# Down projection of a gated MLP with tokens on the partitions, and the residual turned for it

## The chip, the cores and the metric

One core of a Trainium2 chip runs the kernel. Its engines work side by side: PE (matmul; PEld are its weight loads), DVE (VectorE), ACT (ScalarE), POOL (GpSimd) and SP (which issues transfers). The metric is device time in microseconds, the median of three runs.

## The reference, cut to what matters

One encoder layer on 512 tokens of 2048 features, all in float32. The part that the change touches is the end:

```python
x = x + einsum("bsc,cd->bsd", mixed, w_out)          # residual after the mixers
up = einsum("bsd,df->bsf", rms_norm(x, ffn_norm_g), w_up)   # 2048 -> 2 * 5632
gate, val = split(depthwise_conv(up, ffn_dw_w, ffn_dw_b), 2)
x = x + einsum("bsf,fd->bsd", silu(gate) * val, w_down)     # 5632 -> 2048
return rms_norm(x, final_norm_g)      # x * rsqrt(mean(x*x over the 2048) + eps) * g
```

## The kernel before, in words

Everything is kept turned: features on the 128 partitions, the 512 tokens (`S`) along the free axis. `KD` = 16 blocks of 128 features make up a token's 2048. Float32 products are made of three matmuls in a reduced format, with each operand split in a high and a low part (`whi`, `wlo` for weights, `hh`, `hl` for activations): high by high, high by low, low by high. Splitting a 128 x 1024 piece of weights (a *unit*) is one copy on ACT and one subtraction on DVE. Units are loaded by SP into seven buffers (`raw`, `NR` = 7), split into four (`NW` = 4), and asked for three units ahead of their use (`AHEAD` = 3, function `weights`).

The MLP loop runs over `NCH` = 11 groups of `CH` = 4 hidden blocks. Each hidden block `f` is made by seven products (`up`; `pu`), each 8 matmuls of 512 columns and 8 low ones of 256 in one PSUM bank, and by a depthwise convolution and the gate (`hidden`). Between the products stand units of the down projection of the group before (`down`, called after products 3 and 6 through `between`). A unit there is two of the 16 output feature blocks: weights stationary, `hh` and `hl` of 512 tokens moving, four hidden blocks summed in a PSUM bank (`pd`). ACT copies the bank to `pdc`, and POOL adds it to the residual in DRAM by an accumulating transfer (`xd`, shown as `x2d`), 16 feature blocks in all, each [128 features, 512 tokens].

`tick` runs one step of a side job (a Python generator) behind each product; a scheduler then orders each engine's instructions by priority. The order within an engine is fixed when the program is built.

At the end the tenth group's last eight blocks are projected after the last product (`wide`), while the last group's hidden blocks are finished. SP reloads the residual (`reload`, `x2`, lines 830 to 832) and the last weights are split in pieces of 512 columns (`last_weights`, `dh`, `dl`). The eleventh group's projection is done in two halves of 256 tokens (`half`): each adds `pd` to `x2` (L871), squares on ACT (L170), sums the squares over the blocks on DVE (L171). A token's sum of squares then lies across partitions, so `rsqrt_steps` turns it by matmuls with ones (L183), takes the root, and spreads the result over the partitions again with a diagonal and a matmul (L197, L200, `st`). The first half's products with the gain (`finish`, L861) run beside the second half; those of the second half, twelve on DVE and four on POOL, come after it, and eight stores of 256 KB end the program (L862).

Of the kernel before, what the change touches and what calls it, by code (L numbers as in the profile page):

```python
# [16 lines left out]
P = 128  # L17
# [23 lines left out]
H = S // 2  # L41
CH = 4
# [17 lines left out]
         ("nag", NC_), ("g2", KD), ("fww", 2 * NF * 3), ("fwb", 2 * NF), ("g3", KD)]  # L60
# [9 lines left out]
def layer(ctx: ExitStack, tc: tile.TileContext, xT, w_in, w_v, w_out, w_up, w_down, par, tab, out):  # L70
# [94 lines left out]
    def sum_sq(acc, src, first, to=slice(0, S)):  # L165
        if first:
            nc.scalar.activation(acc, src, AF.Square)
        else:
            q = t2("sq")[:, to]
            nc.scalar.activation(q, src, AF.Square)  # L170
            nc.vector.tensor_add(acc, acc, q)  # L171

    def rsqrt_steps(accs, n, name, to=slice(0, S), keep=True, col=None):

        if not isinstance(accs, tuple):
            accs = accs,
        m = (to.stop - to.start) // P
        bank = lambda: (psa.tile([P, 2, S], F32, tag="sc", name="st")[:, 0] if col is None else
                        psa.tile([P, S], F32, tag="po", name="st"))
        ps = bank()  # L180
        for i in range(m):
            for acc in accs:
                nc.tensor.matmul(ps[:, i:i + 1], acc[:, to.start + i * P:to.start + (i + 1) * P], ones[:, 0:1],  # L183
                                 start=acc is accs[0], stop=acc is accs[-1])
        v, r, y = (sm.tile([P, S // P], F32, tag="rs" + c, name="rs" + c)[:, :m] for c in "vry")
        nc.vector.tensor_scalar(v, ps[:, :m], 1.0 / n, EPS, op0=ALU.mult, op1=ALU.add)
# [4 lines left out]
        nc.vector.scalar_tensor_tensor(y, y, 1.5, r, op0=ALU.add, op1=ALU.mult)  # L191
        if col is not None:
            nc.vector.tensor_copy(col, y)
# [6 lines left out]
        nc.tensor.matmul(ps[:, :m * P], ones, dg[:, :m * P], start=True, stop=True)  # L200
        if not keep:
            return ps[:, :m * P]
        res = t2(name)
        nc.scalar.activation(res[:, to], ps[:, :m * P], AF.Copy)
        return res

    def rsqrt_value(g):
        while True:
            try:
                next(g)  # L210
            except StopIteration as e:
                return e.value
# [447 lines left out]
    def down_units(c, i, at):  # L660

        n = U // CH
        if not c:
            return ()
        if c < NCH - 1:
            return {3: (4 * i,), 6: (4 * i + n,)}.get(at, ())
        return {(1, 3): (0,), (1, 6): (2,), (2, 3): (4,), (2, 6): (6,), (3, 6): range(8, KD, n)}.get((i, at), ())

    def down_weights(f0, d0):
        return w_down[:, (f0 * KD + d0 * CH) * P:(f0 * KD + d0 * CH + U) * P]  # L670

    for c in range(NCH):
        for i in range(CH):
            for at, make in enumerate(factors(c * CH + i)):
                plan.append(make)
                for d0 in down_units(c, i, at):
                    plan.append(lambda c=c, d0=d0: unit(down_weights((c - 1) * CH, d0), U * P))

# [122 lines left out]
    def down(hs, ds, wide=False):  # L801

        for d0 in ds:
            w = weights()
            for d in range(d0, d0 + U // CH):

                ps = (psm.tile([P, S], F32, tag="mm", name="pd") if wide and d % 5 > 1 else
                      psa.tile([P, S], F32, tag="tr", name="pd", bufs=2))
                for k in range(CH):
                    mm3(ps, w, (d - d0) * CH + k, *hs[k], k == 0, k == CH - 1)  # L810
                t = t2("pdc")
                nc.scalar.activation(t, ps, AF.Copy)  # L812
                nc.gpsimd.dma_start(xd[d], t, accum_op=ALU.add)  # L813

    pend = None
    for c in range(NCH):
        hs = []
        for i in range(CH):

            last = c == NCH - 1 and i == CH - 1  # L820
            hs.append(hidden(c * CH + i, lambda at: None if last else down(pend, down_units(c, i, at))))
        hs = [in_two(h) for h in hs]
        if not last:
            pend = hs


    n = CH
    x2, ws = [], []

    def reload(d):  # L830
        x2.append(t2("x2"))
        nc.sync.dma_start(x2[d], xd[d])

    def last_weights(d0):
        raw, _ = raw_unit(down_weights(NF - CH, d0), U * P)
        for i in range(2):
            h, l = t2("dh", F32R), t2("dl", F32R)
            o = slice(i * n * P, (i + 1) * n * P)
# [4 lines left out]
    for d in range(KD // 2):  # L843
        reload(d)
    for d in down_units(NCH - 1, CH - 1, 6):
        down(pend, (d,), wide=True)
        last_weights(len(ws))
        last_weights(len(ws))
    for d in range(KD // 2, KD):
        reload(d)  # L850

    def finish(d, r, to, apart=False):

        o = t2("fin").rearrange("p (i t) -> p i t", i=2)
        for i in range(2):
            x, g = x2[d + i][:, to], pc("g3", d + i)
            if apart:
                nc.scalar.activation(x, x, AF.Copy, scale=g)
                nc.gpsimd.tensor_mul(o[:, i], x, r)
# [109 lines left out]
```

## Time and profile before

| | |
|---|---|
| time, median of three runs | 2067.25 us (2064.53, 2067.25, 2067.41) |
| the profiled execution's own time | 2063.7 us |
| its span | 2061.9 us |
| PE busy | 2040.6 us, 99% |
| PEld, DVE, ACT, POOL busy | 1726.8, 1652.3, 1057.5, 156.6 us |
| transfers of `x2d` by POOL | 160 of 256 KB, 4.5 us to landing |
| loads of weights for the MLP | 176 + 88 of 512 KB, 3.6 us to landing |

The span is the profile's; the execution's own time lies 1.8 us above it. Busy time of PE is counted with the overlap of matmuls taken out, so it says that PE was occupied, not that it ran at its peak. The last product of the loop ends at about 1977 us, the last matmul of the projection at 2046.5 us, and what follows is normalisation and stores.

### The profile page before, as it was taken

What the parts mean: (1) busy time and instruction counts of PE and PEld (TensorE: products, weight loads), DVE (VectorE), ACT (ScalarE), POOL (GpSimd) and SP (SyncE); (2) the same over time, 40 slices, a digit from 0 to 9 for tenths busy, and PEclk for the clock granted to TensorE, in tenths of its full rate; (3) what the DMA queues carried; (4) which work ended last, traced back from release to release, by engine and by line L of the source; (5) the groups of instructions that cost most, each with busy time, mean ns of one, the idle gap of its engine ahead of it and who ended that gap; (6) DMA issues with size and microseconds to landing.
All of it is one profiled execution on the core that took longest, in us unless ns stands there. A gap on an engine that the chain in (4) does not pass through costs nothing.

```text
span 2061.9 us, 28498 instructions
## 1 busy us (share of the span) xinstructions
PE 2040.6 (99%) x10746; PEld 1726.8 (84%) x10746; DVE 1652.3 (80%) x2285; ACT 1057.5 (51%) x1714; POOL 156.6 (8%) x186
## 2 busy tenths in 40 slices
PE   9999999999999999999999999999999999999997
PEld 7888888777888998888888888888888888888887
DVE  7798893975577898888888888788788887889876
ACT  7223423466536555555555555555554554555562
POOL 0000000000001001111111111111111111110110
PEclk9999999999999999999999999999999999999998
DMA  6532234325447435555465555555555565554572
GB/s 242 163 103 92 93 115 151 103 72 184 136 144 187 117 123 141 126 143 144 117 150 143 131 135 143 135 131 143 136 134 143 129 144 142 131 137 123 148 210 82
DMA packets 103338, 281.68 MB, mean 137 GB/s; under 512 B 12064, under 2 KB 16672, under 8 KB 103200
## 3 DMA queue, kind: packets, MB, share of 16 engines
q1 hardware_dynamic: 77840, 233.70, 35.7%
q0 software_dynamic: 25216, 46.15, 14.9%
q8 instruction: 85, 1.39, 0.3%
q14 instruction: 53, 0.43, 0.1%
q10 hardware_dynamic: 144, 0.01, 0.0%
HBM read 223.18 MB, written 56.62 MB: 136 GB/s over the span
## 4 chain that ended last, share of the span: by engine, by line
PE 89%; DVE 4%; DMA 3%; issue 2%; ACT 1%; POOL 0%; SPq 0%; DVEq 0%; POOLq 0%; ACTq 0%
PE pu L692 23%; PE pu L693 12%; PE pd L130 8%; PE pd L128 8%; PE pd L129 8%; PE pj L128 5%; PE pj L129 5%; PE pj L130 5%; PE po L128 2%; PE po L129 2%; PE po L130 2%; PE pv L315 1%; PE pv L314 1%; PE pv L316 1%; DMA sq<-sq 1%
## 5 line engine op out<-in xcount | busy, mean ns | idle before, releaser
L692 PE MATMUL pu<-xc,whi 128*128 128x512 f32 x2240 | 782.6, 397 | 0.2 <-ACT pl L706 0.2
L118 DVE TENSOR_TENSOR wlo<-raw,whi 128x1024 fp32r<-128x1024 f32 x364 | 444.7, 1222 | 247.6 <-ACT whi L117 232.1
L117 ACT ACTIVATE whi<-raw 128x1024 fp32r<-128x1024 f32 x364 | 385.1, 1059 | 470.5 <-PE pj L129 130.3
L693 PE MATMUL pu<-xc,wlo 128*128 128x256 f32 x2240 | 583.0, 281 | 0.0
L692 PEld LDWEIGHTS pu<-xc,whi 128*128 128x128 f32 x2240 | 407.8, 188 | 80.3 <-ACT pl L706 0.5
L693 PEld LDWEIGHTS pu<-xc,wlo 128*128 128x128 f32 x2240 | 422.8, 189 | 25.5
L130 PE MATMUL pd<-hh,wlo 128*128 128x512 f32 x640 | 248.9, 391 | 1.4 <-DVE wlo L118 1.4
L128 PE MATMUL pd<-hh,whi 128*128 128x512 f32 x640 | 249.8, 390 | 0.0
L129 PE MATMUL pd<-hl,whi 128*128 128x512 f32 x640 | 249.1, 389 | 0.0
L813 POOL DMA_DIRECT2D x2d<-pdc x160 | 139.6, 874 | 1174.0 <-ACT pdc L812 1072.1
L128 PE MATMUL pj<-xh,whi 128*128 128x512 f32 x512 | 200.5, 396 | 0.2 <-ACT xh L244 0.2
L129 PE MATMUL pj<-xl,whi 128*128 128x512 f32 x512 | 200.4, 391 | 0.1
L130 PE MATMUL pj<-xh,wlo 128*128 128x512 f32 x512 | 200.4, 391 | 0.0
L706 ACT ACTIVATE pl<-pu 128x256 f32<-128x256 f32 x280 | 105.1, 380 | 176.1 <-PE pu L692 176.1
L117 ACT ACTIVATE whi<-ws 128x1024 fp32r<-128x1024 f32 x132 | 139.8, 1059 | 68.5 <-PE pu L692 44.3
L372 DVE SCALAR_TENSOR_TENSOR y<-ch,prm,y 128x510 f32<-128x510 f32 (+14 forms) x240 | 172.0, 743 | 3.5
L118 DVE TENSOR_TENSOR wlo<-ws,whi 128x1024 fp32r<-128x1024 f32 x132 | 161.1, 1220 | 1.4 <-ACT whi L117 1.3
L130 PEld LDWEIGHTS pd<-hh,wlo 128*128 128x128 f32 x640 | 120.1, 188 | 30.0 <-DVE wlo L118 4.9
L812 ACT ACTIVATE pdc<-pd 128x512 f32<-128x512 f32 x160 | 93.9, 588 | 95.4 <-PE pd L130 95.4
L129 PEld LDWEIGHTS pd<-hl,whi 128*128 128x128 f32 x640 | 120.2, 188 | 25.7
L128 PEld LDWEIGHTS pd<-hh,whi 128*128 128x128 f32 x640 | 120.4, 188 | 21.8
L128 PEld LDWEIGHTS pj<-xh,whi 128*128 128x128 f32 x512 | 96.3, 188 | 25.0 <-issue 3.8
(176 smaller groups left out, 2913.7 us busy)
## 6 DMA issues: line engine op xcount, KB each, us to landing
raw<-in_w_up SPq DMA_DIRECT2D x176, 512.0 KB, 3.6
raw<-in_w_down SPq DMA_DIRECT2D x88, 512.0 KB, 3.6
x2d<-pdc POOLq DMA_DIRECT2D x160, 256.0 KB, 4.5
raw<-in_w_in SPq DMA_DIRECT2D x60, 512.0 KB, 3.7
raw<-in_w_out SPq DMA_DIRECT2D x32, 512.0 KB, 3.7
x<-in_xT SPq DMA_DIRECT2D x32, 256.0 KB, 4.3
raw<-in_w_v SPq DMA_DIRECT2D x16, 512.0 KB, 4.8
tab<-in_tab SPq DMA_DIRECT2D x32, 256.0 KB, 4.0
```

The source lines that it names most:

```text
L117: i = nc.scalar.activation(hi[:, :n], raw[:, :n], AF.Copy)
L118: j = nc.vector.tensor_sub(lo[:, :n], raw[:, :n], hi[:, :n].bitcast(F32))
L128: nc.tensor.matmul(ps, hi[:, a], mh, start=start, stop=False)
L129: nc.tensor.matmul(ps, hi[:, a], ml, start=False, stop=False)
L130: return nc.tensor.matmul(ps, lo[:, a], mh, start=False, stop=stop)
L314: nc.tensor.matmul(ps[i], xh, w[0][:, a], start=kk == 0, stop=False)
L372: nc.vector.scalar_tensor_tensor(y[:, a:b], h[:, a + j - PAD:b + j - PAD], prm[:, o + j:o + j + 1], y[:, a:b], op0=ALU.mult, op1=ALU.add)
L692: wide = lambda: nc.tensor.matmul(ps, hi, m, start=k == 0, stop=k == U - 1)
L693: low = lambda: nc.tensor.matmul(ps[:, H:], lo, m[:, :H], start=False, stop=False)
L706: nc.scalar.activation(to, ps, AF.Copy)
L812: nc.scalar.activation(t, ps, AF.Copy)
L813: nc.gpsimd.dma_start(xd[d], t, accum_op=ALU.add)
```

## The change: what it does

The down projection is turned. Hidden activations become the stationary operand, 128 tokens at a time, and 512 columns of weights move; a PSUM bank then holds [128 tokens, 512 features]. The 2048 features are handled in four quarters (`NQ`), four token tiles (`NTT`) each. A quarter takes two units; its four banks are accumulated over both units and copied at the end of the second, and POOL accumulates them into a new DRAM residual `xq[quarter][tile]`. The first group writes `xq` without accumulating.

The residual itself is still made with features on the partitions, so it is turned in a side job, `turn_residual`: per pair of feature blocks SP reloads both, DVE transposes them in blocks of 32 x 32 into one `raw` buffer (`xt`), and SP stores the four bands of 32 partitions to DRAM in runs of 64 elements. The columns of each quarter are chosen (`_quarters`, on the host) so that this regrouping is all that is needed. Then 16 tiles are loaded and accumulated into `xq` by POOL. The job advances with the products of groups 2 to 9.

At the end the tenth group's quarters 2 and 3 are added by DVE straight from PSUM into the reloaded residual, with no copy and no accumulating transfer. The eleventh group goes by token tiles, not by halves: for each quarter DVE adds, ACT squares and accumulates the row's sum in the same instruction, DVE multiplies by the gain (loaded as rows, `g3`). A token's sum is then one number on its partition, so no matmul is needed for the statistics; the root takes the same small steps (`inv_sqrt`), and one scaling per quarter (one on ACT, three on DVE) and one store per quarter finish the tile. The output leaves as [tokens, features] in the quarters' order.

The core of the diff:

```diff
-    def down(hs, ds, wide=False):
-        for d0 in ds:
-            w = weights()
-            for d in range(d0, d0 + U // CH):
-                ps = (psm.tile([P, S], F32, tag="mm", name="pd") if wide and d % 5 > 1 else
-                      psa.tile([P, S], F32, tag="tr", name="pd", bufs=2))
-                for k in range(CH):
-                    mm3(ps, w, (d - d0) * CH + k, *hs[k], k == 0, k == CH - 1)
-                t = t2("pdc")
-                nc.scalar.activation(t, ps, AF.Copy)
-                nc.gpsimd.dma_start(xd[d], t, accum_op=ALU.add)
+    def down3(ps, w, k, hs, kk, i, start, stop):
+        t = slice(i * P, (i + 1) * P)
+        (hi, lo), (h, l) = (x[:, k * S:(k + 1) * S] for x in w[:2]), (x[:, t] for x in hs[kk])
+        nc.tensor.matmul(ps, h, hi, start=start, stop=False)
+        nc.tensor.matmul(ps, h, lo, start=False, stop=False)
+        return nc.tensor.matmul(ps, l, hi, start=False, stop=stop)
+    def down(c, hs, us):
+        for u in us:
+            a, half = divmod(u, 2)
+            w = weights()
+            if not half:
+                both = psa.tile([P, 2, S], F32, tag="sc", name="pd")
+                for j in range(2):
+                    banks.extend([both[:, j], psa.tile([P, S], F32, tag="tr", name="pd", bufs=2)])
+            for i in range(NTT):
+                for k in range(2):
+                    down3(banks[i], w, k, hs, 2 * half + k, i, half == 0 and k == 0, half == 1 and k == 1)
+                if half:
+                    t = t2("pdc")
+                    nc.scalar.activation(t, banks[i], AF.Copy)
+                    if c:
+                        nc.gpsimd.dma_start(xq[a][i], t, accum_op=ALU.add)
+                    else:
+                        nc.gpsimd.dma_start(xq[a][i], t)
...
+    def turn_residual():
+        for m in range(KD // 2):
+            t = t4([P, S // QF, 2, QF], "xt")
+            for e in range(2):
+                xr = t2("xr")
+                nc.sync.dma_start(xr, xd[2 * m + e])
+                for _ in range(3):
+                    yield
+                nc.vector.transpose(t[:, :, e, :], xr.rearrange("p (b j) -> p b j", j=QF))
+            for a in range(NQ):
+                for _ in range(3):
+                    yield
+                p = slice(a * QF, (a + 1) * QF)
+                nc.sync.dma_start(xt[a].rearrange("(b i) f -> i b f", i=QF)[:, :, 2 * m * QF:2 * (m + 1) * QF],
+                                  t[p].rearrange("p b e j -> p b (e j)"))
+        for a in range(NQ):
+            for i in range(NTT):
+                for _ in range(3):
+                    yield
+                t = t2("xr")
+                nc.sync.dma_start(t, xt[a][i * P:(i + 1) * P])
+                for _ in range(2):
+                    yield
+                nc.gpsimd.dma_start(xq[a][i], t, accum_op=ALU.add)
...
+    for a in (2, 3):
+        both = [weights(), weights()]
+        for i in range(NTT):
+            ps = bank()
+            for k in range(CH):
+                down3(ps, both[k // 2], k % 2, pend, k, i, k == 0, k == CH - 1)
+            add(x2[i][a], x2[i][a], ps)
+            last_weights()
+        reload(a - 2)
...
+    for i in range(NTT):
...
+        for a in range(NQ):
+            ps = bank()
+            for k in range(CH):
+                down3(ps, ws[2 * (2 * a + k // 2) + k % 2], 0, hs, k, i, k == 0, k == CH - 1)
+            x = x2[i][a]
+            add(x, x, ps)
+            nc.scalar.activation(t2("sq"), x, AF.Square, accum_out=ssq[:, a:a + 1])
+            fin.append(t2("fin"))
+            nc.vector.tensor_mul(fin[a], x, g3[a])
+            if a == NQ - 2:
+                nc.vector.tensor_reduce(part, ssq[:, :NQ - 1], axis=AX.X, op=ALU.add)
+                nc.vector.tensor_scalar(part, part, 1.0 / D, EPS, op0=ALU.mult, op1=ALU.add)
+        nc.vector.scalar_tensor_tensor(v, ssq[:, NQ - 1:], 1.0 / D, part, op0=ALU.mult, op1=ALU.add)
+        inv_sqrt(y, r, v)
+        for a in range(NQ):
+            to = out[i * P:(i + 1) * P, a * S:(a + 1) * S]
+            if a == 0:
+                nc.scalar.activation(fin[a], fin[a], AF.Copy, scale=y)
+                nc.scalar.dma_start(to, fin[a])
+            else:
+                nc.vector.tensor_scalar(fin[a], fin[a], y, None, op0=ALU.mult)
+                nc.sync.dma_start(to, fin[a])
```

Where instructions stand now. The first place is ACT at the end of a hidden block in the loop: `pl` and `vv` are copies of products, `pdc` of the down projection's banks, `whi` the split of weights, `uy` the convolution's first step. Before:

```order
L706 ACTIVATE pl<-pu 128x256
L812 ACTIVATE pdc<-pd 128x512
L117 ACTIVATE whi<-raw 128x1024
L812 ACTIVATE pdc<-pd 128x512
L780 ACTIVATE uy<-g,prm 128x512
L780 ACTIVATE uy<-vl,prm,fwn 128x512
L706 ACTIVATE vv<-pu 128x256
```

The same place after:

```order
L701 ACTIVATE pl<-pu 128x256
L824 ACTIVATE pdc<-pd 128x512 x4
L775 ACTIVATE uy<-g,prm 128x512
L775 ACTIVATE uy<-vl,prm,fwn 128x512
L120 ACTIVATE whi<-raw 128x1024
L701 ACTIVATE vv<-pu 128x256
```

Four copies now stand in a row, and the split of the next weights has moved from between two copies to behind all four and the convolution's two starts. PE's order in the loop is the same but for the operands.

The second place is SP's queue at the start of the second group. Before, it holds loads of weights alone:

```order
L112 DMA raw<-in_w_up 128x1024 x11
L112 DMA raw<-in_w_down 128x1024
L112 DMA raw<-in_w_up 128x1024
L112 DMA raw<-in_w_down 128x1024
L112 DMA raw<-in_w_up 128x1024 x3
```

After, with the reloads of the residual (`xr`) and the stores of its turned bands (`xt`):

```order
L838 DMA xr<-x2d_4843 128x512
L838 DMA xr<-x2d_4844 128x512
L115 DMA raw<-in_w_down 128x1024
L115 DMA raw<-in_w_up 128x1024 x2
L846 DMA xt_5704<-xt 32x16x64
L115 DMA raw<-in_w_up 128x1024
L115 DMA raw<-in_w_down 128x1024
L115 DMA raw<-in_w_up 128x1024
L115 DMA raw<-in_w_down 128x1024
L846 DMA xt_5705<-xt 32x16x64
```

The turning's six transfers per pair of blocks stand between the loads of weights, each behind what is queued ahead of it.

The third place is DVE after the last product (`hl` and `dl` are low parts of the hidden blocks and of the last weights, `x_...` the reloaded residual). Before:

```order
L798 TENSOR_TENSOR hl<-uy,hh 128x512 x3
L840 TENSOR_TENSOR dl<-raw,dh 128x512 x11
L871 TENSOR_TENSOR x_17741<-x_17741,pd 128x256
L840 TENSOR_TENSOR dl<-raw,dh 128x512
L871 TENSOR_TENSOR x_17743<-x_17743,pd 128x256
L840 TENSOR_TENSOR dl<-raw,dh 128x512 x2
```

After:

```order
L793 TENSOR_TENSOR hl<-uy,hh 128x512 x3
L905 TENSOR_TENSOR x_17861<-x_17861,pd 128x512
L905 TENSOR_TENSOR x_17865<-x_17865,pd 128x512
L905 TENSOR_TENSOR x_17869<-x_17869,pd 128x512
L905 TENSOR_TENSOR x_17873<-x_17873,pd 128x512
L905 TENSOR_TENSOR x_17862<-x_17862,pd 128x512
L887 TENSOR_TENSOR dl<-raw,dh 128x512 x2
L905 TENSOR_TENSOR x_17866<-x_17866,pd 128x512
L887 TENSOR_TENSOR dl<-raw,dh 128x512 x3
L905 TENSOR_TENSOR x_17870<-x_17870,pd 128x512
L887 TENSOR_TENSOR dl<-raw,dh 128x512 x3
L905 TENSOR_TENSOR x_17874<-x_17874,pd 128x512
```

Eight additions, each of which needs a reloaded tile and a filled bank, now stand between and ahead of the splits of the last weights.

More of the change, by code (lines that the diff above doesn't have):

```diff
@@ L41 @@
 H = S // 2
+QF = 32
+NQ = P // QF
+NTT = S // P
 CH = 4
@@ L168, in sum_sq, with inv_sqrt @@
         else:
-            q = t2("sq")[:, to]
+            q = t2("sq")
             nc.scalar.activation(q, src, AF.Square)
             nc.vector.tensor_add(acc, acc, q)
[L173 to L186, printed above, removed]
+    def inv_sqrt(y, r, v):
         nc.scalar.activation(r, v, AF.Sqrt)
@@ L191, in rsqrt_steps @@
         nc.vector.scalar_tensor_tensor(y, y, 1.5, r, op0=ALU.add, op1=ALU.mult)
+    def rsqrt_steps(acc, n, name, col=None):
+        m = S // P
+        bank = lambda: (psa.tile([P, 2, S], F32, tag="sc", name="st")[:, 0] if col is None else
+                        psa.tile([P, S], F32, tag="po", name="st"))
+        ps = bank()
+        for i in range(m):
+            nc.tensor.matmul(ps[:, i:i + 1], acc[:, i * P:(i + 1) * P], ones[:, 0:1], start=True, stop=True)
+        v, r, y = (sm.tile([P, m], F32, tag="rs" + c, name="rs" + c) for c in "vry")
+        nc.vector.tensor_scalar(v, ps[:, :m], 1.0 / n, EPS, op0=ALU.mult, op1=ALU.add)
+        inv_sqrt(y, r, v)
         if col is not None:
@@ L199, in rsqrt_steps @@
         ps = bank()
[L200 to L202 removed]
+        nc.tensor.matmul(ps, ones, dg, start=True, stop=True)
         res = t2(name)
[L204 removed]
+        nc.scalar.activation(res, ps, AF.Copy)
         return res
[L207 to L212, printed above, removed]
     xs, x1 = [], []
@@ L841, in last_weights @@
             ws.append((h, l))
[L843 to L859, printed above, removed]
-            else:
-                nc.vector.scalar_tensor_tensor(o[:, i], x, g, r, op0=ALU.mult, op1=ALU.mult)
-        nc.sync.dma_start(out[d:d + 2, :, to].rearrange("d p t -> p d t"), o)
@@ L900, in layer, with bank @@
-    nc.scalar.activation(rb, r, AF.Copy)
-    for d in range(0, KD, 2):
-        apart = d in (2, 8)
-        finish(d, rb if apart else r, h1, apart)
+    count = [0]
+    def bank():
+        count[0] += 1
+        return (psm.tile([P, S], F32, tag="mm", name="pd") if count[0] % 5 > 1 else
+                psa.tile([P, S], F32, tag="tr", name="pd", bufs=2))
+    for a in (2, 3):
+        reload(a)
+    for a in (2, 3):
+        both = [weights(), weights()]
[6 more added lines that the diff above has]
+        reload(a - 2)
```

103 lines of the change are left out of this document (46 added, 57 removed).

## The prediction, made before the changed kernel ran

> **What bounds the kernel now.** I read the page first (span, busy table, chain of waits), then the windows by stage, then the waits of the long loop, then the timeline of the end.
>
> ```profile
> span 2061.9 us, 28498 instructions
> PE 2040.6 (99%) x10746; PEld 1726.8 (84%) x10746; DVE 1652.3 (80%) x2285; ACT 1057.5 (51%) x1714; POOL 156.6 (8%) x186
> PE 89%; DVE 4%; DMA 3%; issue 2%; ACT 1%; POOL 0%; SPq 0%; DVEq 0%; POOLq 0%; ACTq 0%
> 1200.00:1400.00 200.00, 199.65 (x1043) 169.95 (x1042) 166.45 (x208) 110.87 (x174) 21.78 (x25) 1.00 0.55 133
> 2000.00:2025.00 25.00, 25.00 (x211) 25.00 (x210) 15.31 (x37) 9.33 (x22) 1.00 (x2) 1.00 0.36 88
> 2040.00:2062.00 22.00, 8.38 (x65) 7.56 (x63) 12.23 (x36) 3.10 (x8) 2.79 (x4) 0.74 0.44 145
> ```
>
> The window rows give length, then PE, PEld, DVE, ACT and POOL busy, the granted clock, the DMA share and GB/s. In the loop PE is busy 199.65 us of 200, DVE 166, ACT 111: only PE counts there. In the last projection PE is still full, and PEld is full as well, which it is not in the loop. In the last 22 us PE works 8.4 us: that is the tail. So the change can gain in the last projection and in the tail, and in the loop it can only lose.
>
> ```profile
> ACT whi L117 <- PE pd L129: 114.6, 60, 1.9
> ACT pdc L812 <- PE pd L130: 82.6, 59, 1.4
> DVE raw L642 <- DMA raw<-in_w_up: 0.7, 1, 0.7
> PE pd L130 <- DVE wlo L118: 1.4, 8, 0.2
> ```
>
> These are waits from 900 to 1960 us (total, times, longest). The split of the weights waits for PE to give a buffer back, and for a transfer once, for 0.7 us. PE waits for the split 1.4 us in all. Weights are early; this is the cover for all that the change puts into the loop.
>
> **The last projection.** The timeline gives the pace of the matmuls: of `pd` 512 wide, of `pd` 256 wide, and of `pv`, which already has tokens stationary and weights moving.
>
> ```profile
> 1977.03 0.40 PE L128 MATMUL pd<-hh,whi 128*128 128x512 f32 x1
> 1991.33 0.39 PE L128 MATMUL pd<-hh,whi 128*128 128x512 f32 x1
> 2044.90 0.28 PE L128 MATMUL pd<-hh,dh 128*128 128x256 f32 x1
> 2045.02 0.28 PE L129 MATMUL pd<-hl,dh 128*128 128x256 f32 x1
> 297.25 0.39 PE L316 MATMUL pv<-whi,xl 128*128 128x512 f32 x1
> 297.48 0.39 PE L314 MATMUL pv<-whi,xh 128*128 128x512 f32 x1
> 2023.44 0.79 PE st L183 x8
> 2028.28 0.59 PE st L200 x2
> 2046.22 0.28 PE L130 MATMUL pd<-hh,dl 128*128 128x256 f32 x1
> ```
>
> Starts lie 0.12 us apart at 256 columns and 0.227 at 512 (14.30 us for the 63 steps between the first two rows), not 2:1. Before, 2 halves x 16 blocks x 12 = 384 matmuls take 46.1 us, and the statistics of the first half stand between them (0.79 + 0.59 us). After, 4 token tiles x 4 quarters x 12 = 192 matmuls of 512 take 43.6 us and no `st` matmul is left (46.1 + 1.4 is what lies between 1977.03 + 96 x 0.227 = 1998.8 and the last row's 2046.2, so the two paces account for the stage). PE is done 46.1 + 1.4 - 43.6 = 3.9 us sooner, less 0.1 because the last matmul is longer (0.39 for 0.28): **-3.8 us**. `pv` goes at the same 0.23, so swapping stationary and moving costs nothing per matmul, here or in the loop, where 10 x 192 matmuls stay 192 a group in the same order.
>
> **The tail.** Before, from the last addition:
>
> ```profile
> 2046.54 0.42 DVE L871 TENSOR_TENSOR x<-x,pd 128x256 f32<-128x256 f32 x1 [0.67 <-PE pd L130]
> 2048.43 0.16 DVE L186 TENSOR_SCALAR rsv<-st 128x2 f32<-128x2 f32 x1 [1.14 <-PE st L183]
> 2049.65 0.48 DVE L197 TENSOR_SCALAR dg<-ident,rsy 128x128 f32<-128x128 f32 x2
> 2051.57 4.79 DVE L861 SCALAR_TENSOR_TENSOR fin<-x,prm,st 128x256 f32<-128x256 f32 x12 [1.43 <-ACT rb L900]
> 2054.04 4.02 SPq L862 DMA_DIRECT2D out_T<-fin  x6
> L862 SPq DMA_DIRECT2D out_T<-fin x16: 372/389/674, 2031.0 to 2057.4; - x16
> L585 DVE TENSOR_TENSOR x<-x,po 128x512 f32<-128x512 f32 x16 | 11.0, 686 | 19.2 <-PE po L130 19.2
> L588 ACT ACTIVATE sq<-x 128x512 f32<-128x512 f32 x16 | 10.0, 623 | 2.1 <-DVE x L585 2.1
> L468 ACT ACTIVATION_READ_ACCUMULATOR s<-s,nm 128x1 f32 x64 | 12.1, 189 | 0.0
> L368 DVE TENSOR_SCALAR y<-ch,prm 128x512 f32<-128x512 f32 x8 | 4.4, 544 | 0.2
> ```
>
> Before: 2061.9 - 2046.5 = 15.4 us from that addition to the end: statistics by matmul, diagonal and broadcast up to 2051.57, twelve products until 2056.4, eight stores; the last is issued at 2057.4 and the span ends 4.5 us later. After, the token's sum lies along the free axis: addition 0.69; square with its accumulated sum 0.62 + 0.19 (the product with the gain, 0.69, lies beside it on DVE); variance, root and the four small steps, which took 2049.65 - 2048.43 = 1.22; three scalings of 0.54 = 1.63 with the fourth on ACT; then the 4.5 us from the last issue to the end. Sum 8.9 us: **-6.5 us**. Four stores instead of eight in flight may make the last part shorter (to -8); if the scalings pay the 0.69 of a two-operand addition it is -6.
>
> **The loop, costed at nothing.** (1) Accumulating a quarter over two units makes four banks be copied at the end of the second unit in place of two per unit: the same 16 copies per group. ACT now stands behind a run of four copies, with the split of the next weights behind them; 24 x 0.227 = 5.4 us is a unit, and the loop's period follows from two equal issues of one queue (first two rows; then the copy, the convolution's start, and the weights' load with its time to landing):
>
> ```profile
> 1706.75 0.88 POOL L813 DMA_DIRECT2D x2d<-pdc  x1 [12.41 <-ACT pdc L812]
> 1737.39 0.88 POOL L813 DMA_DIRECT2D x2d<-pdc  x1 [12.42 <-ACT pdc L812]
> L812 ACT ACTIVATE pdc<-pd 128x512 f32<-128x512 f32 x160 | 93.9, 588 | 95.4 <-PE pd L130 95.4
> L780 ACT ACTIVATE uy<-g,prm 128x512 f32<-128x512 f32 x44 | 35.5, 806 | 6.0 <-DVE g L788 6.0
> raw<-in_w_up SPq DMA_DIRECT2D x176, 512.0 KB, 3.6
> ```
>
> 1737.39 - 1706.75 = 30.64 us, less two units, leaves 2.82 us per product. The split is made into four buffers, three units or products ahead: about 8.5 us of cover. What now goes before it after PE's last matmul, the fourth copy and two convolution starts, ends some 2.2 us after PE (0.59 + 2 x 0.81): covered. The bank pair is asked for again four products (11 us) later. (2) The turning adds 16 transposes on DVE. None is in this trace; the nearest rows are one pass over 512 elements, 0.54 (one operand) and 0.69 (two); if it needs two passes, 1.1. That is 9 to 17 us in all, over the 20.6 periods (144 of its steps, 7 a period; 630 us) in which DVE idles some 17%. I take 0.69 each, 11 us, off the path. (3) It adds 64 transfers to SP's queue and 16 accumulating ones to POOL's, which is 8% busy and whose own stores of `pdc` go from 160 to 152; PE waits for none of them. On SP each costs the 0.37 to 0.67 us of an issue, and the loads behind it have the 8.5 us of cover.
>
> (4) The stores of the turned blocks go out in 256-byte runs: 32 transfers x 512. No row has such packets. The nearest:
>
> ```profile
> q1 hardware_dynamic: 3264, 3.15, 43.4%
> q1 hardware_dynamic: 77840, 233.70, 35.7%
> ```
>
> The first is the last 22 us, with 1 KB runs: 0.434 x 22 x 16 / 3264 = 47 ns a packet; the second the whole span: 151 ns. 16,384 packets are then 48 to 155 us of all 16 engines, spread over 630 us: the DMA share of 0.55 rises by 0.08 to 0.25, and by 0.03 for 32 reads of 256 KB (0.357 x 2061.9 x 8.4 / 233.7 MB = 26 us, over the 32 periods in which the turning runs). I take the lower end, as the smaller packet is nearer to it; transfers still find room. The Trainium skill (DMA: Bandwidth & Descriptors, Specifications) asks for at least 512 B for line rate and has smaller writes done as read and modify. No run here shows that yet; by it each store moves twice its bytes and the price is 94 ns and more, which is inside these bounds and changes no sum, but speaks for the rival below that loses time in the loop.
>
> **The hand-over, costed at nothing, with a thin margin.** The eighth to fifteenth blocks of the tenth group were copied by ACT and accumulated by POOL; now DVE adds them straight into reloaded tiles, so PSUM banks come free only when a reload has landed.
>
> ```profile
> 1980.59 3.89 SPq L832 DMA_DIRECT2D x<-x2d  x8
> DMA to landing us min/median/max: 2.7/5.5/6.8
> 1985.32 1.89 DVE L798 TENSOR_TENSOR hl<-uy,hh 128x512 fp32r<-128x512 f32 x3
> L840 DVE TENSOR_TENSOR dl<-raw,dh 128x512 fp32r<-128x512 f32 x16 | 10.2, 687 | 2.5 <-ACT dh L839 2.5
> ```
>
> Reloads go out from 1980.6 and land by about 1991. PE fills a bank in 2.72 us from 1977.0 and needs the sixth at 1990.6; DVE can start adding at 1987.2: 3.4 us to spare. Then the additions stand between the splits of the last weights: five additions, then splits in twos and threes between the others, each addition waiting for its bank. Counting 0.63 us a step (1.89 for three), the last of the 16 splits is done near 2006.7 and PE wants it at 1998.8 + 3 x 2.72 = 2007.0. I take no wait; bounds 0 and 3 us.
>
> **Sum.** -3.8 - 6.5 = -10.3 us. The profiled execution took 2063.7 us, 3.5 below the median of 2067.25 (two of three runs are there, one at 2064.5). From the median that is 2057.0, from the profiled run 2053.4; I say 2056. A run to run spread of this size makes 0.2% (4.1 us) about what can be told from no change.
>
> **Rivals.** *The hand-over waits* (chance 0.14). If reloads land at the 6.8 us maximum or the splits come late, the last projection starts with holes: 3 to 5 us, 2060. For it: the additions now stand ahead of the splits on DVE. Against: in 1975 to 2000 eight accumulating stores disappear.
>
> *The turning starves PE* (0.11, the one that ends slower). Its tile takes one of the seven buffers into which weights are loaded, and its stores stand in SP's in-order queue ahead of loads. Eight rounds: if a round's buffer comes back only when its last store has landed (6.8 us, the longest reload) and the load behind it takes 3.6 us more, PE has 8.5 us of cover and loses 1.9 us; 15 us in eight rounds, net +5: 2072. It decides from 1.3 us a round. For it: loads go out only when a buffer is freed. Against: one transfer wait of 0.7 us in 1060 us.
>
> *Both in part* (0.09): the gain is eaten to within 0.2%, about 2065, for instance by 0.3 us of PE wait in each of the 32 periods in which the turning runs.
>
> **How the numbers follow.** The forecast, nothing waits, has 0.66, with its own range 2051 to 2059 (tail -8 to -6, base 2063.7 or 2067.25). Faster: 0.66 + 0.14 = 0.80; same 0.09; slower 0.11. The range for 8 in 10 runs from 2051 to 2066: below it lies little, above it the slower rival and part of the even one.
>
> **What would show it.** Right: `pd` at 0.227 in the loop and PE at 99.8% there, 1977 to 2043 full, last addition near 2042.7, span near 2051.5. The transposes at 0.5 to 0.7 us. Wrong in the loop: PE or PEld rows that wait for `wlo` or for ACT in the windows of the first eight groups and not in the ninth. Wrong at the hand-over: PE waiting for `dl` or for the reload between 1990 and 2010. Wrong in the tail: more than 9.5 us from the last addition to the end, most likely in stores. What would break the forecast as a whole is a loop that is longer by a fixed amount in each period.

## The result and the profile after

The changed kernel takes 2051.85 us (median of 2050.46, 2050.58, 2053.11 and 2053.19), the kernel before 2066.71 beside it: ratio 0.993, interval 0.9913 to 0.9947, so 14.9 us or 0.7% faster. Run again later with three of the experiments it gave 2048.81 against 2066.22: 0.9919, interval 0.9905 to 0.9933. The forecast was 2056.0 with a range from 2051 to 2066; the first median lies just inside that range, the later one below it. The sign was right and the gain was under-estimated by about 4 us. That the first median lies in the range is in part luck: its lower end left room for a shorter tail and a faster base, not for the gain in the loop that the stages below show.

The page of the profile after: span, busy times, the chain that ended last by engine. Then three windows of the trace after, with the same columns as those of before.

```profile
span 2048.7 us, 28166 instructions
PE 2033.5 (99%) x10534; PEld 1716.5 (84%) x10534; DVE 1657.9 (81%) x2279; ACT 1050.8 (51%) x1707; POOL 155.3 (8%) x190
PE 94%; DMA 2%; DVE 2%; ACT 1%; issue 0%; SPq 0%; DVEq 0%; ACTq 0%
```

```profile
1200.00:1400.00 200.00, 200.00 (x1047) 170.96 (x1046) 168.64 (x214) 109.87 (x173) 21.73 (x25) 1.00 0.61 150
2000.00:2025.00 25.00, 25.00 (x112) 20.72 (x111) 20.04 (x46) 9.86 (x25) 0.00 (x0) 1.00 0.23 88
2027.00:2049.00 22.00, 12.74 (x57) 10.21 (x55) 12.19 (x31) 6.10 (x16) 0.00 (x0) 0.86 0.26 96
```

In the chain, PE has 94% where it had 89: what stood between PE's last work and the end has shrunk. In the last 22 us PE works 12.7 us instead of 8.4. In the last projection PE is still full, with 112 matmul records for 211, and PEld has idle time again. And in the loop PE shows 200.00 us of 200, where it showed 199.65: that the forecast did not have.

Four marks cut each execution into stages: the start of the MLP's first `pu`, of its last `pu`, of the last addition `x<-x,pd`, and the end of the span. PE's rows of the first two, of before and then of after (there the first `pd` behind the last product starts at 1974.28, the time that the expectations name):

```profile
685.65 0.28 PE L128 MATMUL pu<-xc,whi 128*128 128x256 f32 x1
1976.79 0.40 PE L692 MATMUL pu<-xc,whi 128*128 128x512 f32 x1
```

```profile
686.78 0.28 PE L131 MATMUL pu<-xc,whi 128*128 128x256 f32 x1
1974.05 0.40 PE L687 MATMUL pu<-xc,whi 128*128 128x512 f32 x1
```

With the last additions at 2046.54 and 2039.78 and the spans, this gives the table (us); the experiments are cut in the same way. The front runs code that the change leaves alone.

| profiled execution | front | loop | projection | tail | span |
|---|---|---|---|---|---|
| before | 685.65 | 1291.14 | 69.75 | 15.36 | 2061.9 |
| after | 686.78 | 1287.27 | 65.73 | 8.92 | 2048.7 |
| difference | +1.1 | **-3.9** | **-4.0** | **-6.4** | -13.2 |
| after, run again | 683.94 | 1287.31 | 65.73 | 8.92 | 2045.9 |
| `b_order` | 688.99 | 1288.17 | 69.75 | 15.39 | 2062.3 |
| `a_behind` | 686.15 | 1295.10 | 65.73 | 8.52 | 2055.5 |
| `a_noturn` | 686.39 | 1287.40 | 65.73 | 8.68 | 2048.2 |
| `a_narrow` | 687.76 | 1287.55 | 68.28 | 8.91 | 2052.5 |
| `a_dense` | 687.12 | 1291.02 | 65.73 | 8.43 | 2052.3 |
| `a_dense2` | 685.79 | 1287.26 | 65.73 | 8.42 | 2047.2 |
| `a_late` | 684.48 | 1287.15 | 66.18 | 8.99 | 2046.8 |
| `a_tail` | 689.15 | 1286.99 | 65.73 | 8.93 | 2050.8 |
| `a_half` | 685.75 | 1287.87 | 65.73 | 7.65 | 2047.0 |
| `a_split` | 685.64 | 1287.18 | 66.66 | 8.42 | 2047.9 |
| `b_nostat` | 688.96 | 1291.22 | 69.75 | 11.57 | 2061.5 |

The table is a finer measure than the total times. The changed loop, where PE waits for nothing new, takes 1286.99 to 1287.55 us in eight executions and 1287.87 in a ninth; its projection takes 65.73 us eight times, while the front moves by 5 us and the tail by 0.6. So an effect of a microsecond or less is read from the stage, and the total only has to agree with it.

### The profile page after: what moved, and what is told of

It reads as the page before. It is cut to its first block, busy times and chain, and to the rows that moved or that the text cites. A ratio compares the mean times of both kernels' runs of the same rounds, so it can differ in the third digit from the quotient of the medians.

```text
span 2048.7 us, 28166 instructions
## 1 busy us (share of the span) xinstructions
PE 2033.5 (99%) x10534; PEld 1716.5 (84%) x10534; DVE 1657.9 (81%) x2279; ACT 1050.8 (51%) x1707; POOL 155.3 (8%) x190
## 4 chain that ended last, share of the span: by engine, by line
PE 94%; DMA 2%; DVE 2%; ACT 1%; issue 0%; SPq 0%; DVEq 0%; ACTq 0%
PE pu L687 25%; PE pu L688 13%; PE pd L805 8%; PE pd L807 8%; PE pd L806 8%; PE pj L131 5%; PE pj L132 5%; PE pj L133 5%; PE po L131 3%; PE po L132 3%; PE po L133 3%; PE pv L309 1%; PE pv L308 1%; PE pv L310 1%; PE pu L131 1%; PE pu L133 1%
## 5 line engine op out<-in xcount | busy, mean ns | idle before, releaser
L805 PE MATMUL pd<-whi,hh 128*128 128x512 f32 x640 | 250.1, 391 | 0.0
L807 PE MATMUL pd<-whi,hl 128*128 128x512 f32 x640 | 249.5, 390 | 0.0
L806 PE MATMUL pd<-wlo,hh 128*128 128x512 f32 x640 | 249.3, 390 | 0.0
L826 POOL DMA_DIRECT2D xq<-pdc x136 | 119.4, 888 | 828.3 <-ACT pdc L824 743.6
L807 PEld LDWEIGHTS pd<-whi,hl 128*128 128x128 f32 x640 | 120.2, 188 | 25.7
L806 PEld LDWEIGHTS pd<-wlo,hh 128*128 128x128 f32 x640 | 120.3, 188 | 25.2
L805 PEld LDWEIGHTS pd<-whi,hh 128*128 128x128 f32 x640 | 120.4, 188 | 22.1
```

The lines of the kernel that those rows point to most:

```text
L805: nc.tensor.matmul(ps, h, hi, start=start, stop=False)
L806: nc.tensor.matmul(ps, h, lo, start=False, stop=False)
L807: return nc.tensor.matmul(ps, l, hi, start=False, stop=stop)
L826: nc.gpsimd.dma_start(xq[a][i], t, accum_op=ALU.add)
```

## The experiments

### The loop: one split on VectorE (`b_order`, `a_behind`)

The trace of before shows where its loop loses. Three PE rows and two DVE rows at the first of eight such waits, and the waits of PEld from 700 to 1960 us (total, times, longest):

```profile
900.89 0.40 PE L129 MATMUL pd<-hl,whi 128*128 128x512 f32 x1
901.47 0.51 PE L130 MATMUL pd<-hh,wlo 128*128 128x512 f32 x1 [0.18 <-DVE wlo L118]
901.81 0.40 PE L128 MATMUL pd<-hh,whi 128*128 128x512 f32 x1
```

```profile
899.59 0.69 DVE L798 TENSOR_TENSOR hl<-uy,hh 128x512 fp32r<-128x512 f32 x1
900.19 1.22 DVE L118 TENSOR_TENSOR wlo<-raw,whi 128x1024 fp32r<-128x1024 f32 x1
```

```profile
PEld pd L130 <- DVE wlo L118: 4.9, 8, 0.6
```

PE's idle time is given as 0.18 us. But the starts lie 0.58 and 0.34 us apart where the pace is 0.227, so this wait costs 0.35 + 0.11 = 0.46 us: the modelled end of a matmul lies 0.17 us behind the start of the next one, which hides that much of a gap. Eight groups make 3.7 us. The wait is for the low part `wlo` of the first unit's weights, which DVE works on after the third of the group's splits `hl`. In the trace after, the same split stands after the second `hl`; it is done at 901.14 (899.92 + 1.22), PE's first matmul with it starts at 901.44, and PE goes on at its pace:

```profile
899.32 0.69 DVE L793 TENSOR_TENSOR hl<-uy,hh 128x512 fp32r<-128x512 f32 x1
899.92 1.22 DVE L121 TENSOR_TENSOR wlo<-raw,whi 128x1024 fp32r<-128x1024 f32 x1
```

```profile
901.21 0.40 PE L805 MATMUL pd<-whi,hh 128*128 128x512 f32 x1
901.44 0.39 PE L806 MATMUL pd<-wlo,hh 128*128 128x512 f32 x1
```

A likely reason, read from the code and not tested: a unit before sums four hidden blocks, so all the hidden splits were due at once; a first unit after needs two of the four. The text ahead of the prediction calls PE's order the same but for the operands, which is not quite so: before, four matmuls with `whi` (900.19 to 900.89) come ahead of the first with `wlo`; after, `wlo` is in the second. To see whether this place is the cause, the kernel before got the new place, and the changed kernel the old one:

```diff
# b_order, on the kernel before
-        hs = [in_two(h) for h in hs]
+        hs, todo = [], hs
+        for k, h in enumerate(todo):
+            with shifted(40 if k > 1 else 0):       # later in priority
+                hs.append(in_two(h))
# a_behind, on the changed kernel: first unit of a group, not the last group
-                    plan.append(lambda c=c, u=u: unit(down_weights(c - 1, u), U * P))
+                    make = lambda c=c, u=u: unit(down_weights(c - 1, u), U * P)
+                    plan.append(make if u or c == NCH - 1 else lambda make=make: behind_third(make))
...                  # behind_third issues make() behind the third split hl
```

> The kernel before, with the hidden blocks 3 and 4 of each group split later, so that on VectorE the split wlo of a group's first down unit stands ahead of them; nothing else is changed. The split of the time so far: the loop of the changed kernel is about 3.7 us shorter, and in the kernel before PE waits 8 times for wlo at a group's first pd. Theory (the place of that split on VectorE is the cause, 0.46 us for each of 8 groups): the last product then ends 3.7 us sooner, near 1973.3 instead of 1977.0, the 8 waits of PE at pd for wlo are gone or under 0.1 us, and the whole is 3.7 us faster (2063). Rival (the loop gains by the exchange of stationary and moving operands, or by the different banks, and the wait is only where it shows): the last product ends at 1977.0 within 0.7 us.

> The changed kernel, with the split wlo of the first down unit of each group, except the last one, put behind the third of the hidden splits hl on VectorE, where the kernel before has it; nothing else is changed. Theory (the order of that split is what the loop gains): PE waits at the first pd of each group, 0.46 us each, 8 groups, so the last product ends 3 to 3.7 us later, near 1977.5 to 1978.0 instead of 1974.28, and the whole is slower by as much (2055). Rival (operands or banks make the gain): no change of more than 0.7 us.

`b_order` took 2063.47 us against 2066.24, ratio 0.9988 (0.9979 to 0.9997); its loop is 1288.17 us, 2.97 shorter than before. Its profiled execution has a front of 688.99, so the last product ends at 1977.4 and not near 1973.3 as expected; the loop, which the edit concerns, gained 3.0 us of the 3.7 expected. DVE and PE rows of `b_order` at the same place, and its PEld wait:

```profile
902.75 1.22 DVE L118 TENSOR_TENSOR wlo<-raw,whi 128x1024 fp32r<-128x1024 f32 x1
903.89 0.68 DVE L798 TENSOR_TENSOR hl<-uy,hh 128x512 fp32r<-128x512 f32 x1
```

```profile
903.82 0.40 PE L128 MATMUL pd<-hh,whi 128*128 128x512 f32 x1
904.06 0.47 PE L130 MATMUL pd<-hh,wlo 128*128 128x512 f32 x1
904.37 0.39 PE L128 MATMUL pd<-hh,whi 128*128 128x512 f32 x1
```

```profile
PEld pd L130 <- DVE wlo L118: 1.9, 8, 0.2
```

The split is still a little late: PEld waits 0.24 us, no idle time of PE is shown, and the starts are 0.24 and 0.31 us apart, 0.1 us lost. Eight times 0.1 is 0.8 of the 0.9 us by which this loop is still longer than the changed one. The distance from one group to the next says the same without the stages: from the first `pd` with `wlo` near 900 us to the one a group later it is 123.02 us before, 122.66 in `b_order` and 122.56 after.

`a_behind` took 2057.02 us, and its loop is 1295.10: 7.8 us longer than the changed kernel's, twice what was expected. Two DVE rows, PE's first `pd` of `wlo` in the same group, and the waits of PE and PEld from 700 to 1960 us (total, times, longest):

```profile
899.62 1.21 DVE L634 TENSOR_TENSOR ws<-raw 128x1024 f32<-128x1024 f32 x1
901.35 1.21 DVE L121 TENSOR_TENSOR wlo<-raw,whi 128x1024 fp32r<-128x1024 f32 x1
```

```profile
902.62 0.50 PE L813 MATMUL pd<-wlo,hh 128*128 128x512 f32 x1 [0.87 <-DVE wlo L121]
```

```profile
PE pd L813 <- DVE wlo L121: 5.2, 6, 0.9
PEld pd L813 <- DVE wlo L121: 9.1, 9, 1.3
```

The split is late in nine groups, not in eight. In six of them, as in the rows, a scaling of other weights (`ws`, 1.21 us) came in ahead of it too; by the distances between starts each costs 1.15 us, 1.04 before the matmul and 0.11 behind it. In the other three (near 778, 1025 and 1272 us) `ws` is not ahead, PE shows no idle time, and the loss is 0.30 us each. 6 x 1.15 + 3 x 0.30 = 7.8 us, which is the whole difference. Direction and mechanism hold in both kernels, whichever operand is stationary; the rival, that the exchange of operands or the banks speed up the loop, is out, since 3.0 us come without them and what is left has its own wait.

### The turning (`a_noturn`, `a_dense`, `a_dense2`)

```diff
# a_noturn: the side job is not started
-        if c == 1:
-            steps.append(turn_residual())
# a_dense, in turn_residual; also one tick for two before the accumulation
# (a_dense2: range(2) in the three places, nothing else)
-                for _ in range(3):        # three places
+                for _ in range(1):
```

> The changed kernel without the turning of the residual: no transposes, no 64 block stores, no 16 accumulating transfers of it; the residual is not added, so this part of the computation is left out. Theory (the turning is hidden entirely): the last product ends within 0.5 us of 1974.28 and the whole is the same within 0.7 us, although the DMA share in the loop falls from 0.61-0.70 to about 0.55. Rival (contention with the turning costs the loop something everywhere, for instance 0.1 us in each of its 20 periods): 2 us or more faster.

It took 2049.96 us, between the two medians of the changed kernel, and its loop is 1287.40 against 1287.27 and 1287.31. Its window from 1200 to 1400 us (that of after stands first in this document among the windows), and then the row of the hardware's transfer queue (packets, MB, share of 16 engines over the span) of after and of `a_noturn`:

```profile
1200.00:1400.00 200.00, 200.00 (x1047) 170.86 (x1046) 167.18 (x211) 110.04 (x173) 21.78 (x25) 1.00 0.55 137
```

```profile
q1 hardware_dynamic: 97296, 246.28, 40.0%
```

```profile
q1 hardware_dynamic: 75792, 233.69, 36.2%
```

PE is full in both, with the transfer engines at 0.61 in after and 0.55 here. The turning costs nothing that the loop can show.

> The changed kernel with the steps of the turning put closer: one tick of the loop between a step and the next in place of three (and in place of two before an accumulating transfer), so that transposes, block stores and reads come about three times as fast and end about a third of the way through the loop. Theory (weights are 8.5 us ahead, so the turning has room): the loop stays 1287.3 us within 0.5, the whole the same within 0.7 us, though the DMA share there rises above 0.7. Rival (the turning starves PE from 1.3 us a round on; at three times the pace it has no room left): PE waits for wlo or for weights in the eight rounds, 1 to 2 us each, 5 to 15 us slower.

At three times the pace the room ends: the whole took 2051.78 us, with 2048.81 for the changed kernel beside it, and the loop is 3.7 us longer (1291.02). So the theory fails here; but 3.7 us is less than either end of the rival's 5 to 15 us, and comes from one place and not from eight rounds. Two PE rows of `a_dense`, two ACT rows, and windows around them:

```profile
807.93 0.50 PE L687 MATMUL pu<-xc,whi 128*128 128x512 f32 x1 [0.94 <-ACT whi L120]
809.19 0.38 PE L688 MATMUL pu<-xc,wlo 128*128 128x256 f32 x1 [0.76 <-DVE wlo L121]
```

```profile
800.58 1.06 ACT L120 ACTIVATE whi<-ws 128x1024 fp32r<-128x1024 f32 x1 [3.32 <-DVE ws L634]
806.83 2.00 ACT L120 ACTIVATE whi<-raw 128x1024 fp32r<-128x1024 f32 x2
```

```profile
804.00:808.00 4.00, 3.06 (x18) 2.40 (x16) 2.17 (x4) 3.56 (x6) 1.08 (x2) 1.00 1.00 368
809.50:813.20 3.70, 3.70 (x15) 3.17 (x14) 3.70 (x5) 1.88 (x4) 0.00 (x0) 0.56 0.49 141
```

PE shows 0.94 and 0.76 us of waiting; by the distances between starts the two cost about 2.1 us. Then the granted clock falls to 0.56 for 3.7 us, which costs another 1.6 us: together the 3.7 us. The transfer engines are full (1.00, 368 GB/s) in the 4 us ahead of the first wait, but no wait that the trace lists for PE, ACT and DVE from 785 to 811 us is put down to a transfer. PE waits for the split `whi` of 806.83, and ACT reaches it without idle time directly ahead, behind four copies `pdc` and the convolution's two starts; ACT had stood 3.32 us for a scaling `ws` on DVE, and 1.83 us for PE between the second copy and the third. So what the trace shows late is the run of work on ACT. Whether full transfer engines, stores ahead of loads in SP's queue or only another order of the instructions made it late, this run doesn't separate; that stays open.

> The changed kernel with two ticks of the loop between the steps of the turning in place of three, to find where its room ends: at one tick the loop was 3.7 us longer, all of it in one stall of PE at 806 to 813 us. Theory (a stall needs loads that stand behind several stores and a buffer held long, which only the densest pace brings): the loop stays 1287.3 us within 0.3. Rival (the room is used up already at the pace of the change): one or more stalls, the loop 1289 us or more.

2050.35 us, and a loop of 1287.26: no stall. So the room lies between 1.5 and 3 times the pace of the change.

### The hand-over (`a_late`)

```diff
# the reloads in one run, quarters 0 and 1 first
-    for a in (2, 3):
+    for a in range(NQ):
         reload(a)
...
-        reload(a - 2)
```

> The changed kernel with the residual tiles of quarters 0 and 1 reloaded first and those of quarters 2 and 3, which the hand-over needs first, behind them in the queue, as one run of 16 loads: the needed ones go out 8 issues, about 3 us, and their transfer, 2 MB, about 6 us, later. Theory of the prediction (margin of 3.4 us ahead of the first addition, 0.3 us ahead of the last split dl): the additions start near 1991 to 1993 instead of 1987, PE waits 1 to 4 us for a bank near 1990 or for dl near 2007, and the last addition moves from 2039.8 to 2041 or 2044. Rival (the hand-over has more room than the prediction gave it): within 0.5 us of the changed kernel.

It took 2051.57 us; the stage from the last `pu` to the last addition is 66.18 us, 0.45 longer. Of `a_late` the issues, the first additions, and then the same two of after:

```profile
1975.21 9.45 SPq L877 DMA_DIRECT2D x<-xq  x16
1985.04 3.39 DVE L905 TENSOR_TENSOR x<-x,pd 128x512 f32<-128x512 f32 x5 [3.00 <-DMA x<-xq]
```

```profile
1977.63 3.85 SPq L877 DMA_DIRECT2D x<-xq  x8
1984.37 2.48 DVE L905 TENSOR_TENSOR x<-x,pd 128x512 f32<-128x512 f32 x4
1988.10 0.69 DVE L905 TENSOR_TENSOR x<-x,pd 128x512 f32<-128x512 f32 x1 [1.25 <-PE pd L807]
```

Counted from the last `pu` (1971.63 there, 1974.05 in after), the first addition starts at 13.41 us instead of 10.32, now behind a transfer. So the delay was 3.1 us, less than the 4 to 6 expected, and 0.45 of it came through: the margin was about 2.6 us, where the forecast had 3.4. The forecast counted up to the start of the first addition; in `a_late` PE's next matmul starts at 1985.79, when that addition has ended (1985.04 + 0.69), and 3.4 less 0.69 is 2.7. In the kernel as it is, the fifth addition already waits for PE, not PE for it.

### The last projection (`a_narrow`)

```diff
-            for k in range(CH):
-                down3(ps, ws[2 * (2 * a + k // 2) + k % 2], 0, hs, k, i, k == 0, k == CH - 1)
+            for e in (slice(0, H), slice(H, S)):
+                for k in range(CH):
+                    ...          # the three matmuls on ps[:, e], hi[:, e], lo[:, e]
```

> The changed kernel, with each matmul of the last projection done as two of 256 columns, first all of the left half of a bank, then all of the right: 384 matmuls at 0.12 us instead of 192 at 0.227 us. Theory (the last projection's gain is matmul pace, 46.1 against 43.6 us, plus 1.4 us of statistics matmuls that are gone): the stage from the last product to the last addition becomes 2.5 us longer (68.0 instead of 65.5), the tail stays 8.9 us, the whole +2.4 us. Rival (the paces are set by something else, such as the weight load, and the gain came only from the statistics and the hand-over): within 0.5 us of the changed kernel, or more than 4 us longer if the weight loads, now 384 of them, become the limit.

2054.30 us, and the stage is 68.28 us: 2.55 longer than 65.73, with 2.5 expected; loop and tail are untouched. The window 2000 to 2025 us of `a_narrow`:

```profile
2000.00:2025.00 25.00, 25.00 (x210) 25.00 (x210) 19.51 (x44) 8.81 (x21) 0.00 (x0) 1.00 0.25 90
```

PE and PEld are both full, as in the window of before, with the operands of after: it is the width of 256 columns that makes the stage of before slower, not what is stationary. Of the 4.0 us, 2.55 are width; the other 1.5 answer to the 1.4 us of statistics matmuls, which were not tried alone.

### The tail (`b_nostat`, `a_half`, `a_tail`, `a_split`)

The end of the trace after, from the last addition:

```profile
2039.78 0.69 DVE L920 TENSOR_TENSOR x<-x,pd 128x512 f32<-128x512 f32 x1 [0.90 <-PE pd L807]
2040.50 0.63 ACT L921 ACTIVATE sq<-x 128x512 f32<-128x512 f32 x1 [2.00 <-DVE x L920]
2042.47 0.72 ACT L932 ACTIVATE fin<-fin,rsy 128x512 f32<-128x512 f32 x1 [0.81 <-DVE rsy L182]
2042.47 1.28 DVE L935 TENSOR_SCALAR fin<-fin,rsy 128x512 f32<-128x512 f32 x3
2042.98 1.71 SPq L936 DMA_DIRECT2D out_Q<-fin  x3
```

2.69 us from the addition to the first scaling (5.03 before), and 6.23 from there to the end (10.33 before): of the 6.4 us, 2.3 are statistics and 4.1 products and stores.

```diff
# b_nostat, on the kernel before: no statistics of the second half
-    r = rsqrt_value(half(h1, first_half))
+    half(h1, first_half)
     assert not todo
+    r = r0[0]
# a_half
-            to = out[i * P:(i + 1) * P, a * S:(a + 1) * S]
+            n = H if i == NTT - 1 else S
+            to = out[i * P:(i + 1) * P, a * S:a * S + n]
...              # both stores take fin[a][:, :n]
# a_tail
-                nc.sync.dma_start(to, fin[a])
+                (nc.scalar if (i, a) == (NTT - 1, NQ - 1) else nc.sync).dma_start(to, fin[a])
# a_split: for the very last bank only
+            for j, e in enumerate((slice(0, H), slice(H, S)) if end else (slice(0, S),)):
+                ...              # matmuls, addition and square of the columns e
```

> The kernel before, in which the second half of the tokens is scaled by the root of the first half; the statistics of the second half (their matmuls, root, diagonal and broadcast) are left out. Theory (the tail's gain is mainly the chain of statistics: 15.4 us of tail before, 5.0 us of it from the last addition to the first product by the root): the twelve products start near 0.5 us after the last addition, the tail is 10.3 to 10.9 us instead of 15.4, the whole 4.5 to 5 us faster. The rest of the 6.5 us that the change gained in the tail then lies in products and stores. Rival (the products and the eight stores are late for another reason, such as the transfers): the tail stays above 13 us.

Two rows of `b_nostat`:

```profile
2049.93 0.42 DVE L871 TENSOR_TENSOR x<-x,pd 128x256 f32<-128x256 f32 x1 [0.67 <-PE pd L130]
2051.11 4.79 DVE L861 SCALAR_TENSOR_TENSOR fin<-x,prm,st 128x256 f32<-128x256 f32 x12 [0.42 <-ACT rb L902]
```

The products start 1.18 us after the addition (0.5 expected; ACT's square and its copy `rb` still lie there, and DVE waits for `rb`), and the tail is 11.57 us, 3.8 shorter, where 4.5 to 5 were expected; the total is 2062.57 against 2065.47, 0.9985 (0.9975 to 0.9994). Without the statistics 10.4 us are left from the first product on, as before, so the 4.1 us that the change gains there are not the statistics'. The rows put 3.5 of them down to DVE's work, 4.79 us for twelve products and 1.28 for three scalings; that the stores give the rest was not tried alone.

> The changed kernel with the very last store of the output issued from ScalarE's queue, which is idle from 2043.6 us on, in place of third in SyncE's row of three (issued 2042.98 to 2044.69). Theory (the last issue sets the end, since 4.5 us before and 4.0 us after pass from it to the end): the last issue ends near 2044.2 instead of 2044.7, the tail is 8.4 us instead of 8.9. Rival (the four stores of 256 KB share the transfer engines, and their 1 MB sets the end): the tail stays 8.9 us within 0.15.

> The changed kernel, which stores only the first half of each of the last four pieces (0.5 MB in place of 1 MB after the last root; the other half of those rows of the output is left out). The run before showed that issuing the last store 0.5 us sooner moves nothing. Theory (the four stores' bytes through the transfer engines set the end): the tail is about 1.5 us shorter, 7.4 us instead of 8.9. Rival (the time from a store's issue to its landing is nearly fixed, and the first or the last issue sets the end): the tail stays above 8.6 us.

> The changed kernel with the very last bank computed in two halves of 256 columns, each added and squared by itself, so that the first half's addition and square lie beside the second half's matmuls; a trial of a kernel that beats both. Theory (the chain from the last matmul to the root sets the end): addition 0.42 for 0.69 us and square 0.42 for 0.63, against 12 x (0.24 - 0.227) = 0.16 us more on PE: last addition to end 8.4 us instead of 8.9, the whole 0.3 us shorter, seen in the stages only. Rival (the small steps and their waits for each other are the chain, and they do not shrink): the same within 0.1 us.

`a_tail` (2051.30 us) has 8.93 us of tail, with its last issue earlier; but kernels with the same ending show 8.42 to 8.99 us, so half a microsecond can't be judged from it, and it is inconclusive; it does not show that an earlier issue moves nothing, as the expectation of `a_half` has it. `a_half` (2050.08) has 7.65 us, 0.8 to 1.3 under those of that spread, in one execution: bytes count, though probably less than the 1.5 us expected. Medians from issue to landing in `a_half`, whole and half pieces:

```profile
out_Q<-fin SPq DMA_DIRECT2D x9, 256.0 KB, 3.1
out_Q<-fin SPq DMA_DIRECT2D x3, 128.0 KB, 2.2
```

`a_split` (2051.57) is no better than the changed kernel: its tail of 8.42 lies inside the spread, and the stage ahead of it became 0.93 us longer, since PE waits for the first half's addition before it writes the other half of the bank:

```profile
2037.74 0.39 PE L923 MATMUL pd<-dh,hh 128*128 128x256 f32 x1 [0.51 <-DVE x L926]
```

No version that beats the changed kernel came out of this.

## Why the prediction was right, and where it was wrong

**Last projection, -3.8: right.** 4.0 by the stages, 2.55 of it shown to be width.

**Tail, -6.5: right.** 6.4. Addition to scaling took 2.69 us (2.72 forecast). Behind it two errors cancel, which is luck: the three scalings took 1.28 us instead of 1.63, since starts lie closer than one instruction's time, and from their end 4.95 us pass instead of 4.5.

**Loop, costed at nothing: wrong, and this is the step that failed.** "In the loop it can only lose" was drawn from windows with PE at 199.65 of 200. The prediction had the row of the eight waits for `wlo` before it, 1.4 us in all, and used it only as a proof that weights are early. It missed twice: it did not ask whether the change moves that split, and it took 1.4 us for the price, where the distances between starts say 3.7. `b_order` gives 3.0 of the 3.9 us in the kernel before by this move alone. With this term the sum would have been -14.0 against -14.3 by the stages.

**Turning, costed at nothing: right.** Transposes took 705 ns (0.69 assumed). Against `a_noturn`, q1 has 40.0% of 2048.7 us less 36.2% of 2048.2 us, 78 us of all engines; less the 26 us that the prediction gives its reads, 16,384 packets of 256 bytes would take 52 us, 51 ns each. This is an estimate, and `after` is its high end: q1 of `a_behind`, with the same transfers, has 38.0% of 2055.5 us, which gives 13 ns. Both are near or under the lower bound of 47 that was taken, and far from 151. The Trainium skill (DMA: Bandwidth & Descriptors, Specifications) has writes below 512 B done as read and modify. By twice the bytes the 47 ns would become 94 ns and more, an estimate that this case does not bear out.

**Rival "turning starves PE": did not happen.** At 1.5 times the pace there is still no stall. At three times PE stalls once, at the start, and not once a round; the trace shows work on ACT as what it waits for, so the rival's mechanism, loads held up by buffers and stores, is not shown.

**Hand-over: right, with less margin.** No wait; about 2.6 us to spare instead of 3.4, because the bank comes free at the end of an addition and not at its start.

**Base.** The prediction chose 2056 between 2057.0 from the median and 2053.4 from the profiled execution. The 3.5 us between these are within what the front moves by (below), but only the faster of those executions has a trace.

## What to carry to other kernels

Where an engine is over 99% busy, price the remaining waits by the distance between starts, not by the idle time shown: eight waits shown as 0.18 us cost 0.46 each. When a change alters which inputs a step needs, follow the splits that stand around it on the helper engine; a shift of one place there was worth about as much as the redesigned last projection. And measure a small effect by stages cut at the same instructions, since the untouched front moved by more than most of the effects here.

## What the runs showed of the hardware

Part of the front's movement comes in steps. Windows from 436 to 450 us, of after run again, of after and of `b_order`, and then a narrower one of `b_order`:

```profile
436.00:450.00 14.00, 12.10 (x70) 9.29 (x70) 8.63 (x21) 9.07 (x19) 0.00 (x0) 1.00 0.25 89
```

```profile
436.00:450.00 14.00, 11.98 (x60) 8.93 (x59) 6.42 (x17) 6.77 (x16) 0.00 (x0) 0.88 0.31 102
```

```profile
436.00:450.00 14.00, 11.59 (x52) 8.83 (x50) 6.32 (x17) 6.21 (x15) 0.00 (x0) 0.76 0.23 76
```

```profile
440.00:445.00 5.00, 5.00 (x28) 4.16 (x28) 2.30 (x12) 4.92 (x11) 0.00 (x0) 0.50 0.00 0
```

The clock granted there, just after PE waited some 2 us for statistics, is 1.00, 0.88 or 0.76, and the fronts are 683.94, 686.78 and 688.99 us. The narrower window shows half clock (0.50). The 0.12 that is missing from 14 us is 1.7 us, half of 3.4: one stretch of 3.4 us at half clock, or two where 0.24 is missing. That accounts for 1.7 and 3.4 of the 2.8 and 5.1 us between these fronts; the rest is not traced. All fourteen executions show one of the three values: 1.00 in four, with fronts of 683.94 to 685.65 us, 0.88 in six, with 685.75 to 687.12, and 0.76 in four, with 687.76 to 689.15. In `a_dense` 0.94 and 0.76 us of waiting were followed by one such stretch. The Trainium skill (TensorE: Matmul & The Clock Gate, Part 1: The HAM clock gate) has the clock halved after an idle window of about 3.4 us. The length agrees, but here the clock fell after shorter waits, of 2.0 us in after and 2.4 us in `b_order`, and did not after one of 2.35 us in the execution of before. So the length of the wait alone does not decide it, and what does stays open. A short stall of PE can so cost more than its own length, as the 1.6 us of clock in `a_dense` show.
